# A two-layer encoder trunk on one core: small on-chip tiles allocated next to each other, so that the large tiles share one start residue modulo 512 bytes

## The chip, the cores and the metric

The kernel runs on one core of a Trainium2 chip, as one program with one launch. The metric is device microseconds for the whole program, median of three runs. TensorE (PE) multiplies, ScalarE (ACT) and VectorE (DVE) prepare and post-process, GpSimd (POOL) does a few small operations, and SyncE (SP) issues most DMAs. All tiles that the engines share lie in the on-chip memory SBUF, 128 partitions wide. An address in this text is the byte at which a tile starts inside each partition, and its residue is that address modulo 512.

## What is computed

Two layers (`L = 2`), sequence 256, width 2048. Each layer normalises `x`, projects it by a 2048 x 14784 matrix, runs four branches on the columns, and merges them:

```
for l in range(DEPTH):
    h = _rms_norm(x, norm_g[l])
    p = h @ w_in[l]
    ...                                  # split p into the inputs of four branches
    y_a = _rwkv7_bidir(...)              # bidirectional recurrent mixing
    y_b = _diff_attention(...)           # differential attention with a bias by distance
    y_c = _mla(...)                      # attention from low-rank latents
    y_d = _mem_attention(m_q, rms_norm(mem) @ mem_w_kv[l], ...)
    for bi, y in enumerate((y_a, y_b, y_c, y_d)):
        zb = sigmoid(merges[:, :, bi]) * ((y * silu(gates[:, :, bi])) @ w_branch[l, bi])
        z = zb if z is None else z + zb
    x = x + z @ w_out[l]
```

All of it is in float32, so the large products are made in three parts (below).

## The kernel before

**Main stream.** `main` (L564) walks a fixed list of jobs (`jobs`, L491). A job is one block of at most 512 weight columns: `mem_w_kv`, `w_in` (30 blocks), the latent up-projections, `w_branch`, `w_out`. For every 128 rows of a block, `prepare` loads the weights into `raww` (three buffers of 4096 bytes, two row groups each; SP issues the DMA), and `split` (L166) makes two float32r tiles from it: ACT copies to `whi`, DVE subtracts to `wlo` (five buffers each of 512 columns, 2048 bytes). The activations are split in the same way, once per use: `T1h`/`T1l` (high and low part of the normalised `x`, 16 slices of 256 columns), `ygh`/`ygl` (branch outputs), `S0` to `S7` (memory tokens), and for `w_out` a set of eight tiles that hold `z` in slices, in the order `X`, `iA`, `BK` with `qr`, `q1`, `T1h`, `k1`, `T1l`, `V1` (`z_prep`, L797). `product` (L624) then issues three matmuls: high x high, high x low, low x high.

**Which operand stays and which streams.** In most jobs (`tpos` false) the activation slice, 128 x 128, is loaded as the stationary operand, and 512 weight columns stream past it. In the jobs for the recurrent inputs and the gates (`tpos` true) a 128 x 128 slice of the weights is stationary, and 256 activation columns stream. A stationary slice is 512 bytes per partition, so that all slices of a tile start at the tile's own residue. In the trace the name before the comma is the streamed tile, the one behind it the stationary one: `mm<-whi,T1h` streams `whi` past a slice of `T1h`. The trace leaves the number off names, so `q` is `q1` and `k` is `k1`.

**Side work.** The branches, the norms and the tables run as generators that `build` (L1496) interleaves with the main stream by estimated engine clocks; their float32 matmuls go to the PSUM tags `pa` and `pr`.

**Where tiles lie.** A pool places tags in the order in which each is first used, one behind the other, each rounded up to 32 bytes. Before the change small tags lie between large ones: `small` (6 buffers of 64 bytes), `gains` (128 bytes), `cols` (476), `mrs` (8), `xss` (32), `bm` (256). `small(n)` (L181) hands out one of its buffers for row sums and softmax statistics; `rsqrt` (L176) runs on POOL with the constant -0.5 from `cst`.

| tile (use) | bytes | start before | residue before | start in the changed build | residue |
|---|---|---|---|---|---|
| whi, wlo (weights) | 2048 each | 91072 to 109504 | 448 | 91776 to 110208 | 128 |
| raww | 4096 each | 78784 | 448 | 79488 | 128 |
| T1l, T1h, V1 | 16384, 16384, 4096 | 112032, 135584, 151968 | 416 | 112256, 135808, 152192 | 128 |
| X, S0 to S7, ygh | 4096 each, 5120 | 20288, 24384, 69440 | 320 | 21120, 25216, 70272 | 128 |
| q1 | 4096 | 74688 | 448 | 75392 | 128 |
| k1, iA, BK, ygl, qr | 4096, 4096, 2048, 5120, 2048 | 181984, 199392, 197344, 203488, 220896 | 224 | 181888, 199296, 197248, 203392, 220800 | 128 |

Of the kernel before, what the change touches and what calls it, by code (L numbers as in the profile page):

```python
# [10 lines left out]
F32 = mybir.dt.float32  # L11
F32R = mybir.dt.float32r
I32 = mybir.dt.int32
U8 = mybir.dt.uint8
# [12 lines left out]
O_U, O_DQ, O_DK, O_DV, O_LAT, O_MQ, O_G, O_M = 0, 1792, 2304, 2816, 3328, 4032, 4544, 6592  # L27


C_ID, C_MF, C_MB, C_BLK, C_CEN, C_B2, C_MH, C_IF, C_OH, C_N = (  # L30
    0, 128, 256, 384, 512, 640, 642, 658, 690, 694)


P_SH, P_W0, P_A0, P_KK, P_KA, P_RK, P_GG, P_GB = 0, 42, 50, 58, 62, 66, 70, 74
P_DQ, P_DK, P_DS, P_QL, P_KL, P_NP, P_MM, P_N = 78, 79, 80, 81, 84, 86, 88, 90
# [18 lines left out]
def _constants():  # L54
    c = np.zeros((128, C_N), np.float32)
    c[:, C_ID:C_ID + 128] = np.eye(128)
    s = np.arange(128)[:, None] % 64
    t = np.arange(64)[None, :]
    c[:, C_MF:C_MF + 64] = s < t
    c[:, C_MF + 64:C_MF + 128] = s <= t  # L60
    c[:, C_MB:C_MB + 64] = s > t
    c[:, C_MB + 64:C_MB + 128] = s >= t
    blk = (np.arange(128)[:, None] // 64 == np.arange(128)[None, :] // 64).astype(np.float32)
    c[:, C_BLK:C_BLK + 128] = blk
    c[:, C_CEN:C_CEN + 128] = np.eye(128) - blk / 64
    c[:, C_B2:C_B2 + 2] = blk[:, [0, 64]]
    c[:, C_MH:C_MH + 16] = -0.5
    c[:, C_IF:C_IF + 32] = (10000.0 ** (-np.arange(0, 64, 2) / 64.0))[None, :]
    p = np.arange(128)
    g = p // 16 % 4  # L70
    c[p, C_OH + np.where(p < 64, g, 3 - g)] = 1.0
    return c
# [40 lines left out]
class Builder:  # L113
# [65 lines left out]
        self.nc.gpsimd.tensor_tensor(ss, ss, self.cst[:, C_MH:C_MH + n], op=ALU.pow)  # L179

    def small(self, n):  # L181
        return self.t("small", [128, 16], bufs=6)[:, :n]


    def setup(self):
        nc, a = self.nc, self.a
        self.cst = self.cp.tile([128, C_N], F32, name="cst")
        self.ident = self.cst[:, C_ID:C_ID + 128]
        self.G = [self.cp.tile([128, 2, 4, 65], F32, name=f"G{i}") for i in range(2)]
        self.ticks = [nc.gpsimd.memset(self.G[0], 1.0).ins]  # L190
        self.ones = self.cp.tile([128, 2], F32, name="ones")
        nc.gpsimd.memset(self.ones, 1.0)
        with self.tc.high_priority(2 * HP):
            nc.scalar.activation(self.small(2), self.ones, AF.Exp)
            warm = self.t("PT", [128, 2, 256], bufs=1)[:, 0]
            nc.vector.memset(warm, 0.0)
            ps = self.pa()[:, :256]
            for i in range(4):
                self.nc.tensor.matmul(ps, lhsT=warm[:, :128], rhs=warm, start=True, stop=True)
        self.TT = [self.cp.tile([128, 2, 4, 64], F32, name=f"TT{i}") for i in range(2)]  # L200
        self.ticks.append(nc.gpsimd.memset(self.TT[0], 0.0).ins)
        self.ST = [[self.cp.tile([128, 2, 2, 64], F32, name=f"ST{u}{i}") for i in range(2)] for u in range(2)]
        for s in self.ST[0]:
            at = nc.gpsimd.memset(s, 0.0).ins
        self.ticks.append(at)
        pace = self.t("X", [128, 1024])
        for i in range(6):
            with self.tc.issue_after(self.ticks[-1]):
                self.ticks.append(nc.gpsimd.memset(pace[:, i % 2 * 512:i % 2 * 512 + 512], 0.0).ins)
        with self.tc.issue_after(self.ticks[-1]):  # L210
            nc.gpsimd.memset(self.G[1], 1.0)
            for s in (self.TT[1], *self.ST[1]):
                nc.gpsimd.memset(s, 0.0)
        self.biasd = self.dr.tile([4, 128, 2, 256], F32, name="biasd")
        self.x1d = self.dr.tile([128, 2, 2048], F32, name="x1d")
# [925 lines left out]
    def rw_prep(self, l, ft, U, pos):  # L1141

        nc, a = self.nc, self.a
        cols = self.v["cols", l]
        cst = self.cst
# [3 lines left out]
        def col(p):  # L1149
            return cols[:, p:p + 1]  # L1150

        b2 = cst[:, C_B2:C_B2 + 2]
        wup = self.t("wup", [128, 2, 128], bufs=1)
        aup = self.t("aup", [128, 2, 128], bufs=1)
        fs = slice(ft * 128, ft * 128 + 128)
# [41 lines left out]
        for d in range(2):  # L1197
# [48 lines left out]
            for n in range(3):  # L1246
                c = 3 - n if d else n
# [99 lines left out]
    def rw_finish(self, l, ft, U, unit):  # L1347

        nc, cst = self.nc, self.cst
        cols = self.v["cols", l]  # L1350
        v = U[:, 8 + ft]
        kds, sq, yg = unit[4], *unit[-2:]
        b2 = cst[:, C_B2:C_B2 + 2]

        def col(p):
            return cols[:, p:p + 1]

        ps = self.pr()
        for tt in range(2):
            self.mm(ps[:, 2 * tt:2 * tt + 2], sq[:, tt * 128:tt * 128 + 128], b2)  # L1360
        var = self.small(4)
        nc.vector.tensor_scalar(var, ps[:, 0:4], 1.0 / 64, GN_EPS, op0=ALU.mult, op1=ALU.add)
        nc.gpsimd.tensor_tensor(var, var, cst[:, C_MH:C_MH + 4], op=ALU.pow)
        yield
        ex = self.t("sq", [128, 4, 64])
        nc.vector.tensor_copy(ex, var[:, :, None].to_broadcast([128, 4, 64]))
        bs = self.pr()[:, :256]
        self.mm(bs, cst[:, C_BLK:C_BLK + 128], kds)
        bv = self.t("r4", [128, 256], bufs=1)
        nc.vector.tensor_tensor(bv, bs, v, op=ALU.mult)  # L1370
        yield
        ps = self.pr()[:, :256]
        for tt in range(2):
            self.tr(ps[:, tt * 128:tt * 128 + 128], ex[:, 2 * tt:2 * tt + 2].rearrange("p a b -> p (a b)"))
        nc.vector.scalar_tensor_tensor(yg, yg, col(P_GG + ft), ps, op0=ALU.mult, op1=ALU.mult)
        nc.vector.scalar_tensor_tensor(U[:, ft], yg, col(P_GB + ft), bv, op0=ALU.add, op1=ALU.add)
        yield
# [250 lines left out]
```

## Time and profile before

| | |
|---|---|
| time of the kernel, median of 3 runs | 2039.71 us (2037.15 to 2041.34) |
| time of the profiled execution | 2037.85 us |
| its span, first to last instruction | 2036.1 us |
| PE busy | 2012.8 us, 99% of the span |
| DVE, ACT, POOL busy | 1433.0, 1114.3, 147.9 us |
| DMA traffic | 367 MB, 180 GB/s over the span |

A matmul row gives a modelled duration, since matmuls overlap: one of 512 columns is listed with some 395 ns, yet the next starts some 233 ns later. The pace of PE is therefore read from start to start, in the timeline, and not from the durations. In the timeline a line with x2 or x3 stands for that many instructions of one kind that follow each other, and its first number is the start of the first.

### The profile page before, as it was taken

To read this page: it belongs to the slowest core of one execution; us is meant where nothing else is said; L and a number is where in the kernel's file an instruction comes from. 1 tells how busy PE (TensorE), PEld (TensorE's weight loads), DVE (VectorE), ACT (ScalarE), POOL (GpSimd) and SP (SyncE) were. 2 spreads that over 40 slices of the span, in tenths; PEclk is the share of its full clock that TensorE was granted. 3 is DMA by queue.
4 is the path that set the end of the run, shared out by engine and by line. 5 is a ranking of instruction groups with operands and counts; after the bars stand their busy time and mean duration, and the time that the engine had idled before them with its cause. 6 is when DMAs were issued, how large, how long until landed. Compare 5 with 4: busy or idle time off the path is not lost.

```text
span 2036.1 us, 33810 instructions
## 1 busy us (share of the span) xinstructions
PE 2012.8 (99%) x12054; PEld 1688.6 (83%) x12054; DVE 1433.0 (70%) x3134; ACT 1114.3 (55%) x2293; POOL 147.9 (7%) x178
## 2 busy tenths in 40 slices
PE   9899999999999999999999999999999999999999
PEld 7798997778877877888889989987788878788887
DVE  6888898877787865648565658775577777565564
ACT  6756576455455544555465565755555554454443
POOL 1101112001100000100000000110011100000000
PEclk9899999999999999999999999999999999999999
DMA  8555655545565655765766656564556555456565
GB/s 275 181 177 160 196 179 179 171 136 159 166 203 168 181 164 158 222 189 191 243 191 181 186 151 192 166 194 140 151 172 187 173 169 180 150 168 200 185 197 187
DMA packets 222313, 367.34 MB, mean 180 GB/s; under 512 B 40576, under 2 KB 60800, under 8 KB 221824
## 3 DMA queue, kind: packets, MB, share of 16 engines
q1 hardware_dynamic: 218752, 356.31, 57.6%
q10 hardware_dynamic: 3168, 8.39, 1.1%
q8 instruction: 94, 1.54, 0.3%
q0 software_dynamic: 224, 0.49, 0.2%
q14 instruction: 75, 0.61, 0.1%
HBM read 357.78 MB, written 11.53 MB: 181 GB/s over the span
## 4 chain that ended last, share of the span: by engine, by line
PE 92%; DMA 3%; DVE 3%; issue 1%; ACT 1%; SPq 0%; POOL 0%; DVEq 0%; ACTq 0%; POOLq 0%
PE mm L156 82%; PE pr L156 5%; PE pa L156 2%; PE pa L161 2%; DVE wlo L95 1%; DMA raww<-in_w_in 1%; DMA raww<-in_mem_w_kv 1%; PE pr L161 0%; ACT whi L95 0%; DMA TT<-yd 0%; DVE half L95 0%; DVE BK L95 0%; DVE U L95 0%; DMA sc<-S 0%; DVE sq L95 0%
## 5 line engine op out<-in xcount | busy, mean ns | idle before, releaser
L95 DVE TENSOR_TENSOR wlo<-raww,whi 128x512 fp32r<-128x512 f32 (+2 forms) x1300 | 863.9, 674 | 468.8 <-ACT whi L95 463.8
L95 ACT ACTIVATE whi<-raww 128x512 fp32r<-128x512 f32 (+2 forms) x1300 | 789.7, 617 | 731.1 <-PE mm L156 538.0
L156 PE MATMUL mm<-whi,T1l 128*128 128x512 f32 (+2 forms) x1472 | 573.4, 392 | 0.0
L156 PE MATMUL mm<-wlo,T1h 128*128 128x512 f32 (+2 forms) x1440 | 569.6, 396 | 1.3 <-DVE wlo L95 1.1
L156 PE MATMUL mm<-whi,T1h 128*128 128x512 f32 (+2 forms) x1472 | 533.3, 394 | 1.6 <-ACT whi L95 1.6
L156 PEld LDWEIGHTS mm<-whi,T1h 128*128 128x128 f32 x1472 | 274.9, 188 | 62.8 <-ACT whi L95 2.3
L156 PEld LDWEIGHTS mm<-whi,T1l 128*128 128x128 f32 x1472 | 276.4, 188 | 58.6 <-issue 0.7
L156 PEld LDWEIGHTS mm<-wlo,T1h 128*128 128x128 f32 x1440 | 270.2, 188 | 62.5 <-DVE wlo L95 3.9
L156 PE MATMUL mm<-T1l,whi 128*128 128x256 f32 x960 | 271.9, 284 | 4.7 <-DVE T1l L95 4.7
L156 PE MATMUL mm<-T1h,whi 128*128 128x256 f32 x960 | 271.6, 284 | 2.3 <-ACT T1h L95 2.3
L156 PE MATMUL mm<-T1h,wlo 128*128 128x256 f32 x960 | 272.2, 285 | 0.4 <-DVE wlo L95 0.4
L156 PEld LDWEIGHTS mm<-T1l,whi 128*128 128x128 f32 x960 | 182.4, 190 | 5.6 <-DVE T1l L95 5.0
L156 PEld LDWEIGHTS mm<-T1h,whi 128*128 128x128 f32 x960 | 182.3, 190 | 3.1 <-ACT T1h L95 2.5
L156 PEld LDWEIGHTS mm<-T1h,wlo 128*128 128x128 f32 x960 | 182.0, 190 | 1.0 <-DVE wlo L95 0.8
L156 PE MATMUL mm<-wlo,ygh 128*128 128x512 f32 (+1 forms) x296 | 117.0, 397 | 0.0
L156 PE MATMUL mm<-whi,ygl 128*128 128x512 f32 (+1 forms) x296 | 115.7, 392 | 0.0
L156 PE MATMUL mm<-whi,ygh 128*128 128x512 f32 (+1 forms) x296 | 112.7, 400 | 0.0
L156 PE MATMUL mm<-whi,S 128*128 128x512 f32 x256 | 84.9, 408 | 2.6 <-ACT whi L95 2.1
L179 POOL TENSOR_TENSOR small<-small,cst 128x4 f32<-128x4 f32 (+3 forms) x45 | 52.0, 1157 | 395.1 <-DVE small L95 375.7
L156 PEld LDWEIGHTS mm<-whi,ygh 128*128 128x128 f32 x296 | 55.4, 188 | 12.3 <-issue 0.7
L156 PEld LDWEIGHTS mm<-whi,ygl 128*128 128x128 f32 x296 | 55.7, 188 | 11.9 <-issue 0.3
L156 PEld LDWEIGHTS mm<-wlo,ygh 128*128 128x128 f32 x296 | 55.7, 188 | 11.2 <-issue 0.7
(319 smaller groups left out, 2173.0 us busy)
## 6 DMA issues: line engine op xcount, KB each, us to landing
raww<-in_w_in SPq DMA_DIRECT2D x432, 512.0 KB, 3.6
raww<-in_w_branch SPq DMA_DIRECT2D x64, 512.0 KB, 4.3
raww<-in_w_out SPq DMA_DIRECT2D x64, 512.0 KB, 4.5
raww<-in_mem_w_kv SPq DMA_DIRECT2D x29, 512.0 KB, 4.2
raww<-in_w_in SPq DMA_DIRECT2D x16, 384.0 KB, 3.3
raww<-in_w_in SPq DMA_DIRECT2D x16, 320.0 KB, 3.6
raww<-in_w_in SPq DMA_DIRECT2D x16, 256.0 KB, 2.7
Z<-in_mem ACTq DMA_DIRECT2D x2, 1024.0 KB
```

The source lines that it names most:

```text
L95: return g(out, *args, **kw)
L156: return self.nc.tensor.matmul(out, lhsT=lhsT, rhs=rhs, start=start, stop=stop).ins
L161: self.nc.tensor.transpose(out, in_, self.ident[:k, :k])
L179: self.nc.gpsimd.tensor_tensor(ss, ss, self.cst[:, C_MH:C_MH + n], op=ALU.pow)
```

## The change

The constant tile `cst` loses two columns that held a pair of 0/1 block columns (`b2`, now read from the block matrix with a step of 64 columns) and eight of the sixteen columns of -0.5. It shrinks from 694 to 684 columns. `small` has five buffers in place of six. In `setup` the tags `gains`, `cols`, `mrs`, `xss` and `bm` and the first `small` are requested once, before any large tile, and so they lie together ahead of `PT`. From `PT` on, every tile starts at residue 128.

```
-C_ID, C_MF, C_MB, C_BLK, C_CEN, C_B2, C_MH, C_IF, C_OH, C_N = (
-    0, 128, 256, 384, 512, 640, 642, 658, 690, 694)
+C_ID, C_MF, C_MB, C_BLK, C_CEN, C_MH, C_IF, C_OH, C_N = (
+    0, 128, 256, 384, 512, 640, 648, 680, 684)
...
-    c[:, C_B2:C_B2 + 2] = blk[:, [0, 64]]
-    c[:, C_MH:C_MH + 16] = -0.5
+    c[:, C_MH:C_MH + 8] = -0.5
...
     def small(self, n):
-        return self.t("small", [128, 16], bufs=6)[:, :n]
+        return self.t("small", [128, 16], bufs=5)[:, :n]
...
         nc.gpsimd.memset(self.ones, 1.0)
+
+        for tag, n, dt in (("gains", 32, F32), ("cols", P_N + 29, F32), ("mrs", 2, F32), ("xss", 8, F32),
+                           ("bm", 256, U8)):
+            self.t(tag, [128, n], dt)
+        self.small(2)
...
-        b2 = cst[:, C_B2:C_B2 + 2]
+        b2 = cst[:, C_BLK:C_BLK + 128:64]
```

The last edit stands in `rw_prep` and in `rw_finish`. The tiles requested in `setup` have no instruction of their own. In the built programs each engine issues the same instructions in the same order before and after, with the same operands by name; only the DMA of `cst` is 10 columns shorter. PE, DVE and SP also wait for the same things at the same places. On ACT and POOL 37 waits differ, all at instructions that write a `small` tile or follow one that does, since five buffers come round sooner than six.

## Rows read from the trace of the kernel before

**Rows 1.** The page, part 1: engine, busy us (share), instructions.

```profile
PE 2012.8 (99%) x12054; PEld 1688.6 (83%) x12054; DVE 1433.0 (70%) x3134; ACT 1114.3 (55%) x2293; POOL 147.9 (7%) x178
```

**Rows 2.** The page, part 4: the chain that ended last, by engine and line.

```profile
PE 92%; DMA 3%; DVE 3%; issue 1%; ACT 1%; SPq 0%; POOL 0%; DVEq 0%; ACTq 0%; POOLq 0%
PE mm L156 82%; PE pr L156 5%; PE pa L156 2%; PE pa L161 2%; DVE wlo L95 1%; DMA raww<-in_w_in 1%; DMA raww<-in_mem_w_kv 1%; PE pr L161 0%; ACT whi L95 0%; DMA TT<-yd 0%; DVE half L95 0%; DVE BK L95 0%; DVE U L95 0%; DMA sc<-S 0%; DVE sq L95 0%
```

**Rows 3.** Waits: who waited for whom, us in total, times, longest.

```profile
ACT whi L95 <- PE mm L156: 538.0, 671, 3.7
...
ACT whi L95 <- DMA raww<-in_w_in: 99.0, 74, 5.3
...
ACT E L95 <- DVE small L95: 28.0, 19, 5.2
```

**Rows 4.** Groups by shape: line engine op, out<-streamed,stationary, xcount | busy us, mean ns | idle.

```profile
L156 PE MATMUL mm<-whi,T1l 128*128 128x512 f32 x1344 | 531.7, 399 | 0.0
L156 PE MATMUL mm<-wlo,T1h 128*128 128x512 f32 x1312 | 526.5, 401 | 1.3 <-DVE wlo L95 1.1
L156 PE MATMUL mm<-whi,T1h 128*128 128x512 f32 x1344 | 493.4, 400 | 0.9 <-ACT whi L95 0.9
...
L156 PE MATMUL mm<-T1h,wlo 128*128 128x256 f32 x960 | 272.2, 285 | 0.4 <-DVE wlo L95 0.4
...
L156 PE MATMUL mm<-wlo,ygh 128*128 128x512 f32 x272 | 109.0, 401 | 0.0
L156 PE MATMUL mm<-whi,ygl 128*128 128x512 f32 x272 | 107.2, 395 | 0.0
L156 PE MATMUL mm<-whi,ygh 128*128 128x512 f32 x272 | 105.0, 405 | 0.0
L156 PE MATMUL mm<-whi,S 128*128 128x512 f32 x256 | 84.9, 408 | 2.6 <-ACT whi L95 2.1 <-ACT S L95 0.4
...
L156 PE MATMUL mm<-wlo,S 128*128 128x512 f32 x128 | 52.3, 409 | 0.0
```

**Rows 5.** Timeline, PE in layer 0's `w_out`: start us, us, engine line op, names, xcount.

```profile
946.91 0.62 PE L156 MATMUL mm<-whi,q 128*128 128x512 f32 x2
...
949.64 0.63 PE L156 MATMUL mm<-whi,T1h 128*128 128x512 f32 x2
...
953.32 0.62 PE L156 MATMUL mm<-whi,k 128*128 128x512 f32 x2
...
963.10 0.64 PE L156 MATMUL mm<-whi,X 128*128 128x512 f32 x2
963.58 0.40 PE L156 MATMUL mm<-wlo,X 128*128 128x512 f32 x1
...
967.30 0.63 PE L156 MATMUL mm<-whi,BK 128*128 128x512 f32 x2
...
970.10 0.62 PE L156 MATMUL mm<-whi,q 128*128 128x512 f32 x2
...
972.85 0.63 PE L156 MATMUL mm<-whi,T1h 128*128 128x512 f32 x2
```

**Rows 6.** Groups by shape, PE, 936.7 to 1043 us (layer 0's `w_out`).

```profile
L156 PE MATMUL mm<-whi,X 128*128 128x512 f32 x32 | 10.9, 395 | 0.0
...
L156 PE MATMUL mm<-whi,k 128*128 128x512 f32 x32 | 10.7, 394 | 0.0
L156 PE MATMUL mm<-whi,q 128*128 128x512 f32 x32 | 10.6, 391 | 0.0
```

**Rows 7.** Timeline, PE in a job that streams 256 activation columns.

```profile
123.89 0.28 PE L156 MATMUL mm<-T1l,whi 128*128 128x256 f32 x1
...
126.97 0.28 PE L156 MATMUL mm<-T1h,whi 128*128 128x256 f32 x1
```

**Rows 8.** Groups by shape, DVE.

```profile
L95 DVE TENSOR_TENSOR wlo<-raww,whi 128x512 fp32r<-128x512 f32 x1192 | 812.0, 690 | 435.1 <-ACT whi L95 430.6
...
L95 DVE TENSOR_TENSOR Z<-Z,sg 128x512 f32<-128x512 f32 x32 | 22.2, 692 | 0.2
```

**Rows 9.** The tile `sq`: the matmuls with `b2`, duration ns min/median/max.

```profile
L156 PE MATMUL pr<-cst,sq x32: 165/251/272, 140.3 to 1604.5; 128*128 128x2 f32 x32
```

More of the change, by code (lines that the diff above doesn't have):

```diff
@@ L1352, in rw_finish @@
         kds, sq, yg = unit[4], *unit[-2:]
-        b2 = cst[:, C_B2:C_B2 + 2]
+        b2 = cst[:, C_BLK:C_BLK + 128:64]
         def col(p):
```

## The prediction

> **What bounds the kernel now.** I read the busy table first: PE is busy 99% of the span, DVE 70%, ACT 55% [rows 1]. Since matmul durations are modelled, that alone doesn't show a bound, so I went on to the chain of work that ended last: 92% of it is PE, and 82% is the one line that issues the weight products [rows 2]. The waits say the same from the other side: the longest in total is ACT's, 538.0 us for a `whi` buffer that PE hasn't released yet [rows 3]. The weights are ready ahead of PE nearly everywhere. So the time is the number of products by the distance from one start to the next, and a change that moves neither instructions nor waits on PE can act only through that distance. The reader should therefore look at the start times of the products, and at what tells a slow distance from a fast one.
>
> **What the starts show.** In `w_out` the same `whi` and `wlo` tiles stream past eight sets of stationary slices in turn, 12 products a set, all of one shape and with no wait. From the first product of `k` to the first of `BK` there are five sets (`k`, `T1l`, `V`, `X`, `iA`), 60 products, in 967.30 - 953.32 = 13.98 us [rows 5], or 233.0 ns each. The set of `q` takes 949.64 - 946.91 = 2.73 us, and in the next pass 972.85 - 970.10 = 2.75 us [rows 5]: 227.5 and 229.2 ns each, 228.3 on average. The modelled durations of that stage agree in sign: 391 ns for `q`, 394 for `k`, 395 for `X` [rows 6]. What sets `q1` apart is its address: it alone begins at residue 448, the residue of `whi` and `wlo` that stream past it. The five others begin at 416, 320 and 224, and whichever of these it is, the set comes out at about 233. I read this as the two reads of PE, the stream of the current product and the load of the next stationary slice, getting in each other's way a little unless both start at the same place modulo 512. After the change every product has such a pair.
>
> **The change, part by part.**
>
> Products of 512 columns. The eight rows of this shape hold 1344 + 1312 + 1344 + 3 x 272 + 256 + 128 = 5,200 [rows 4]. `w_out` has 2 layers x 4 blocks x 16 slices x 2 halves x 3 = 768; 160 of them already stand in the rows of `T1h` and `T1l`, and 96 are those of `q1`, which have equal residues already. That leaves 5,200 + 768 - 160 - 96 = 5,712 products that change. Each should go from 233.0 to 228.3 ns: 4.7 ns x 5,712 = 26.8 us. Ends: 3 ns by the modelled durations of `q` and `k` [rows 6], 17 us; 5.5 ns by the better pass of `q`, 31 us.
>
> Products of 384 and 320 columns (456 in the latent blocks) have the same operands and shorter streams: 1 us.
>
> Products of 256 columns: 3 x 960 = 2,880 [rows 4]. Here the weight slice, residue 448, is stationary, and `T1h` or `T1l`, residue 416, streams. 26 of them start within 126.97 - 123.89 = 3.08 us [rows 7], 118.5 ns each. No row shows this shape with equal residues. At the share of the long ones (4.7 of 233.0, 2%) they would save 2.4 ns each, 6.9 us; at the least they save nothing, and at the most the same 4.7 ns, 13.5 us. A loss can't be excluded by a row either (the rival below prices it). I take half of the share, 1.2 ns, 3.5 us.
>
> The rest. DVE and ACT may read and write at any of these residues: DVE's operation of 512 elements takes 690 ns where all three tiles lie at 448 and 692 ns where they lie at 448 and 224 [rows 8], so that sharing a residue costs or gives DVE nothing. The two-column matmuls with `b2` number 32, at a median of 251 ns [rows 9]; reading their two columns 256 bytes apart may change them by some tens of ns each, 1 us together either way, beside work of other lanes. I take 0. With five `small` buffers, 37 waits on ACT and POOL differ. Nothing is queued on PE behind them directly; behind an ACT one stands the next `whi`, and PE holds whole `whi` buffers ahead (the 538.0 us). All of ACT's waits of softmax exponentials for DVE's statistics are 28.0 us in total today [rows 3]; if that grew by a tenth, 3 us on ACT, PE would see little of it. I take 0, and 3 us as its end. The shorter DMA of `cst` is nothing.
>
> What comes late next. The gain is 26.8 + 1 + 3.5 = 31 us, 1.5% of PE's pace. ACT has 45% of the span free and DVE 30% [rows 1], so they can follow. Some waits remain and don't shrink: 8% of the chain is not PE [rows 2], among it DMA at 3%, and ACT waits 99.0 us for weights still on their way [rows 3]. Where such a wait ends last, a faster PE only arrives earlier. I take a tenth of the gain back, 3 us: 28 us remain.
>
> Sum, against the profiled execution: 2037.85 - 28 = 2010. It lies 1.9 us under the median of the runs shown, so the time I give is 2012. Its own ends: a gain of 17 less a fifth is 14 us, 2026; a gain of 31 + 1 + 13.5 is 45 us, 1994.
>
> **A rule against it.** The starts differ by 4.7 ns between `q1` and the rest [rows 5], in the same stage, with the same streamed tiles. The Trainium skill (SBUF — State Buffer, Who interferes with whom) says that PE has two independent read ports, one for the moving operand and one for LDWEIGHTS, and that PE never waits on anyone. By that rule the residue is worth nothing and the time stays at 2040; by the row it is worth 28 us. The trace speaks against the rule, as far as one tile out of eight can.
>
> **The rivals.**
>
> No change. Then `q1` would be fast for another reason: it lies next to `raww` and nearer to `whi` than any other set does, or the order of the sets favours it. For it: only one tile of eight has equal residues, and it has one place. Against it: `wlo` lies 10 KB further than `whi`, and both kinds of product sit in the sets that I timed; `X`, `V` and `k` lie at very different distances and are alike. The products keep 233 ns and `small` and `b2` remain: 2037 to 2042, say 2040. By the page's rule above it comes out here as well. Chance 0.21.
>
> Slower. Equal residues keep the two reads in step for the whole stream, and in step could mean in conflict every time. The rows hold such a pace: two products of `X` take 963.58 - 963.10 = 0.48 us, 240 ns each [rows 5]. At 240 in place of 233, 5,712 products cost 40 us more: 2080. It decides as soon as the mean distance of the 512-column products is above 233.0. Against it stands `q1`, which has equal residues and the lowest pace; for it, that the residue itself will be 128 and no longer 448, which no pair of the trace has. With a 240 on a part of the products only, it ends between 2044 and 2080. Chance 0.14.
>
> Given back. PE's pace improves as forecast, but the feed of weights takes half of it: ACT already waits 74 times for `raww` from `w_in` [rows 3], with only three `raww` buffers. 2037.85 - 15 + 1.9 = 2025. Against it: the 538.0 us in which ACT waits for PE are five times as much. Chance 0.10.
>
> **How the numbers follow.** The forecast, 2012 with its own ends 1994 and 2026, gets 0.55. Forecast and half gain together make faster 0.65. No change is 0.21; slower is 0.14. About 0.2% (4 us) is what a measurement of this kernel can tell from no change. The range reaches from 1994 over the half gain to the no-change case at 2042, and leaves out the slower case (0.14) and a few hundredths below.
>
> **What would show it.** In the profile after, every set of `w_out` should take 2.72 to 2.76 us from its first product to the first of the next, and no longer only `q`'s; the groups of 512 columns should be listed some 3 to 5 ns shorter, `T1h` and `T1l` above all; the 256-column products should start 116 to 118.5 ns apart; DVE's 690 ns should stay. If the sets still take 2.79 while `q` does too, the residue was not the cause and the rival of no change holds. If `q` stays fast and the others don't follow, equal residues are not enough. If the sets take 2.73 and the time stays, the gain was given back, and ACT's waits for `raww` must have grown.

## The result and the profile after

The changed kernel takes **2016.39 us** (median of 4 runs, 2015.58 to 2017.52) against 2038.82 us of the kernel before (median of 4 runs beside it, 2037.15 to 2041.34): a ratio of 0.9889, 95% interval 0.9872 to 0.9906. The forecast was 2012, faster. The profiled execution took 2015.58 us, 22.3 us less than that of before; its span fell by the same amount, from 2036.1 to 2013.8 us.

The page of the kernel after, busy line and chain, as [rows 1] and [rows 2]. Line numbers are one lower than before (L155 is the matmul that was L156):

```profile
PE 1990.4 (99%) x12054; PEld 1693.6 (84%) x12054; DVE 1431.4 (71%) x3134; ACT 1111.5 (55%) x2293; POOL 149.2 (7%) x178
...
PE 93%; DVE 3%; DMA 2%; issue 1%; ACT 0%; POOL 0%; SPq 0%; DVEq 0%; ACTq 0%; POOLq 0%
```

The instruction counts are the same, PE is as full as before, and PE's busy time alone is 22.4 us shorter. Nothing was taken off the chain; its steps became shorter. The waits of after, as [rows 3] (who waited for whom: us in total, times, longest):

```profile
ACT whi L94 <- PE mm L155: 406.1, 496, 6.5
...
ACT whi L94 <- DVE wlo L94: 132.5, 180, 1.7
...
ACT whi L94 <- DMA raww<-in_w_in: 98.6, 73, 3.8
...
ACT E L94 <- DVE small L94: 29.1, 19, 5.4
...
PE mm L155 <- ACT whi L94: 3.2, 4, 1.5
```

Two of these rows before, which [rows 3] does not show:

```profile
ACT whi L95 <- DVE wlo L95: 21.1, 28, 2.1
...
PE mm L156 <- ACT whi L95: 3.8, 4, 1.5
```

ACT's wait for PE to release a `whi` is 132 us shorter, but 111 us of that stand under DVE's `wlo` now: the profile puts a wait for several engines down to the one that came last. The rows of PE and of `wlo` together went from 559.1 to 538.6 us, 20.5 less. PE itself waits for `whi` and `wlo` 4.6 us in total (5.3 before), so the feed still keeps up. ACT's wait for `raww` from `w_in` (99.0 before) and the one for `small` (28.0 before) have hardly moved; over all weights, ACT's waits for `raww` went from 134.1 to 140.8 us.

PE in layer 0's `w_out` after, as [rows 5] (start us, us, engine line op, names, xcount):

```profile
944.42 0.62 PE L155 MATMUL mm<-whi,k 128*128 128x512 f32 x2
...
958.02 0.62 PE L155 MATMUL mm<-whi,BK 128*128 128x512 f32 x2
...
960.74 0.62 PE L155 MATMUL mm<-whi,q 128*128 128x512 f32 x2
...
963.46 0.62 PE L155 MATMUL mm<-whi,T1h 128*128 128x512 f32 x2
```

From the first product of `k` to the first of `BK` the same 60 products take 13.60 us where they took 13.98: 226.7 ns each, not 233.0. The set of `q` takes 2.72 us and no longer stands out. The groups by shape after, as [rows 4] (us in total, modelled mean ns):

```profile
L155 PE MATMUL mm<-whi,T1l 128*128 128x512 f32 x1344 | 525.5, 394 | 0.0
...
L155 PE MATMUL mm<-T1h,wlo 128*128 128x256 f32 x960 | 274.5, 287 | 0.0
...
L155 PE MATMUL mm<-whi,ygl 128*128 128x512 f32 x272 | 106.4, 392 | 0.0
...
L155 PE MATMUL mm<-whi,S 128*128 128x512 f32 x256 | 82.3, 399 | 2.5 <-ACT whi L94 2.5
```

The groups of 512 columns in [rows 4] lost 3 to 10 ns by their modelled durations, those with `S` most. The group of 256 columns **gained** 2 ns. The timeline of a job with 256 columns after, as [rows 7], says the same by its starts: 26 products in 127.03 - 123.91 = 3.12 us, 120.0 ns each, where it was 118.5.

```profile
123.91 0.28 PE L155 MATMUL mm<-T1l,whi 128*128 128x256 f32 x1
...
127.03 0.28 PE L155 MATMUL mm<-T1h,whi 128*128 128x256 f32 x1
```

DVE's operation of 512 elements and the 32 matmuls with `b2`, as [rows 8] and [rows 9], did not move (690 ns and 251 ns before):

```profile
L94 DVE TENSOR_TENSOR wlo<-raww,whi 128x512 fp32r<-128x512 f32 x1192 | 811.5, 691 | 420.0 <-ACT whi L94 415.6 <-PE mm L155 0.5
```
```profile
L155 PE MATMUL pr<-cst,sq x32: 165/251/272, 138.1 to 1589.1; 128*128 128x2 f32 x32
```

**The whole account.** A mean *pace* in the rest of this text is the distance from the start of a product to the next start on PE, over all products of one width that are followed directly by another product. Distances above 256 ns (512 columns) or 128 ns (256 columns), 5% and 3% of them, are left out as interrupted. Number of distances, their sum and their mean:

| | 512 columns | 256 columns |
|---|---|---|
| before | 5,317, 1238.5 us, 232.9 ns | 2,759, 326.4 us, 118.3 ns |
| after | 5,312, 1210.4 us, 227.9 ns | 2,750, 329.6 us, 119.9 ns |

So 28.1 us went out of the long products and 3.2 us came back in the undisturbed short ones (1.6 ns on all 2,880 are 4.5 us). All starts from product to whatever follows add up to 1832.2 us before and 1808.4 after, 23.8 less. The span fell by 22.3, so 1.5 us came back outside the products.

### The profile page after: what moved, and what is told of

It is laid out like the page before. It is cut to its first block, busy times and chain, and to the rows that moved or that the text cites. A ratio compares the mean times of both kernels' runs of the same rounds, so it can differ in the third digit from the quotient of the medians.

```text
span 2013.8 us, 33812 instructions
## 1 busy us (share of the span) xinstructions
PE 1990.4 (99%) x12054; PEld 1693.6 (84%) x12054; DVE 1431.4 (71%) x3134; ACT 1111.5 (55%) x2293; POOL 149.2 (7%) x178
## 3 DMA queue, kind: packets, MB, share of 16 engines
q10 hardware_dynamic: 3168, 8.39, 1.2%
## 4 chain that ended last, share of the span: by engine, by line
PE 93%; DVE 3%; DMA 2%; issue 1%; ACT 0%; POOL 0%; SPq 0%; DVEq 0%; ACTq 0%; POOLq 0%
PE mm L155 84%; PE pr L155 5%; PE pa L155 3%; PE pa L160 2%; DVE wlo L94 1%; DMA U<-in_memT 1%; DMA raww<-in_mem_w_kv 0%; PE pr L160 0%; DMA TT<-yd 0%; DVE BK L94 0%; DMA raww<-in_w_in 0%; DMA BK<-sp 0%; DVE half L94 0%; ACT whi L94 0%; DVE U L94 0%
## 5 line engine op out<-in xcount | busy, mean ns | idle before, releaser
L155 PE MATMUL mm<-whi,T1l 128*128 128x512 f32 (+2 forms) x1472 | 567.2, 388 | 0.0
L155 PE MATMUL mm<-wlo,T1h 128*128 128x512 f32 (+2 forms) x1440 | 564.8, 392 | 1.4 <-DVE wlo L94 1.4
L155 PE MATMUL mm<-whi,T1h 128*128 128x512 f32 (+2 forms) x1472 | 527.8, 391 | 0.7 <-ACT whi L94 0.7
L155 PEld LDWEIGHTS mm<-whi,T1h 128*128 128x128 f32 x1472 | 275.3, 188 | 55.9 <-ACT whi L94 2.0
L155 PEld LDWEIGHTS mm<-whi,T1l 128*128 128x128 f32 x1472 | 276.9, 188 | 51.8 <-issue 0.7
L155 PEld LDWEIGHTS mm<-wlo,T1h 128*128 128x128 f32 x1440 | 270.8, 188 | 58.1 <-DVE wlo L94 5.3
L155 PE MATMUL mm<-T1l,whi 128*128 128x256 f32 x960 | 274.1, 286 | 4.7 <-DVE T1l L94 4.7
L155 PE MATMUL mm<-T1h,whi 128*128 128x256 f32 x960 | 273.8, 286 | 2.3 <-ACT T1h L94 2.3
L155 PE MATMUL mm<-T1h,wlo 128*128 128x256 f32 x960 | 274.5, 287 | 0.0
L155 PEld LDWEIGHTS mm<-T1l,whi 128*128 128x128 f32 x960 | 185.9, 194 | 5.5 <-DVE T1l L94 5.0
L155 PEld LDWEIGHTS mm<-T1h,whi 128*128 128x128 f32 x960 | 185.8, 194 | 3.0 <-ACT T1h L94 2.5
L155 PEld LDWEIGHTS mm<-T1h,wlo 128*128 128x128 f32 x960 | 185.5, 194 | 0.4
L155 PE MATMUL mm<-wlo,ygh 128*128 128x512 f32 (+1 forms) x296 | 116.0, 393 | 0.0
L155 PE MATMUL mm<-whi,ygl 128*128 128x512 f32 (+1 forms) x296 | 114.9, 389 | 0.0
L155 PE MATMUL mm<-whi,ygh 128*128 128x512 f32 (+1 forms) x296 | 111.7, 397 | 0.0
L155 PE MATMUL mm<-whi,S 128*128 128x512 f32 x256 | 82.3, 399 | 2.5 <-ACT whi L94 2.5
L155 PEld LDWEIGHTS mm<-whi,ygh 128*128 128x128 f32 x296 | 55.3, 188 | 11.4 <-issue 0.7
L155 PEld LDWEIGHTS mm<-whi,ygl 128*128 128x128 f32 x296 | 55.6, 188 | 11.0 <-issue 0.3
L155 PEld LDWEIGHTS mm<-wlo,ygh 128*128 128x128 f32 x296 | 55.6, 188 | 10.6 <-issue 0.7
```

What stands on the lines that cost most here:

```text
L155: return self.nc.tensor.matmul(out, lhsT=lhsT, rhs=rhs, start=start, stop=stop).ins
```

## Experiments

The theory to be tested: PE's pace in the 512-column products is set by the difference between the start residues of the weights and of the other operand. Below, **D** is the residue at which the weights start minus that of the other tile, modulo 512. Before, D is 32 for `T1h`, `T1l` and `V1`, 128 for `X`, `S` and `ygh`, 224 for `k1`, `iA`, `BK`, `qr` and `ygl`, and 0 for `q1` alone. After, it is 0 everywhere. The rivals: that one of the other edits (`small`, `b2`, `cst`) does it, or the residue 128 itself.

**E1, the placement alone**, in the kernel before: six `small`, the long `cst` and the old `b2` stay; every large tile comes to residue 224, not 128.

```
         nc.gpsimd.memset(self.ones, 1.0)
+        for tag, n, dt in (("gains", 32, F32), ("cols", P_N + 29, F32), ("mrs", 2, F32), ("xss", 8, F32),
+                           ("bm", 256, U8)):
+            self.t(tag, [128, n], dt)
+        self.small(2)
```

> The kernel before with the six requests in setup alone: six small buffers, the long constants and the two columns of b2 stay. Every tile from PT on then starts at residue 224, which is not a multiple of 64. Theory (the difference between the residue of the streamed tile and that of the stationary tile sets the pace): 512-column products start 226 to 228 ns apart in all eight sets of w_out, and the time is that of the changed kernel, 2016 us, within 3. Rival (the residue 128 itself, or starts on multiples of 128 bytes): the pace stays at 233 ns and the time at 2039 us. Rival (small, constants or b2 did it): 2039 us too.

Measured: 2019.42 us (2018.37 to 2022.86), 0.9906 of before [0.9889, 0.9922]; 227.8 and 119.9 ns. PE in `w_out` of this kernel:

```profile
948.68 0.62 PE L156 MATMUL mm<-whi,k 128*128 128x512 f32 x2
...
962.28 0.62 PE L156 MATMUL mm<-whi,BK 128*128 128x512 f32 x2
```

60 products in 13.60 us, as in the kernel after. The time is 0.4 us beyond the expected band, but the ratio agrees with that of the kernel after (0.9889 [0.9872, 0.9906]). The gain is in the placement, and the residue 128 has no part in it.

**E2, all the rest**: the kernel after without the five lines above, so that every D is as before.

```
-        for tag, n, dt in (("gains", 32, F32), ...):
-            self.t(tag, [128, n], dt)
-        self.small(2)
```

> The changed kernel without the requests in setup: five small buffers, short constants, b2 read with a step. All tiles from PT on move by the same 96 bytes against before, so that their residues differ as before (streamed weights 352, q1 352, T1h 320, X 224, k1 128). Theory: sets of w_out at 233 ns a product, q alone near 228, 2039 us within 3. Rival (small, constants or b2 did it): 2016 us.

Measured: 2039.73 us, 0.9996 of before [0.9985, 1.0007]; 233 and 118.3 ns. In its `w_out`:

```profile
950.50 0.62 PE L155 MATMUL mm<-whi,q 128*128 128x512 f32 x2
...
953.23 0.63 PE L155 MATMUL mm<-whi,T1h 128*128 128x512 f32 x2
...
956.91 0.62 PE L155 MATMUL mm<-whi,k 128*128 128x512 f32 x2
...
970.89 0.63 PE L155 MATMUL mm<-whi,BK 128*128 128x512 f32 x2
```

13.98 us for the 60 products and 2.73 us for `q`, both as before. The residue of every large tile has moved by 96 bytes, no difference has, and `q` is still the one fast set. `small`, `b2` and `cst` are worth nothing that can be measured.

**E3 and E4, ten differences in one kernel.** On top of the kernel after, each of the ten weight buffers gets its own tag and starts 32 bytes further in its residue than the one ahead of it. In E3 the `whi` have D = 0 to 128 and the `wlo` 160 to 288; in E4, 192 to 320 and 352 to 480. One `Rs` in place of two makes the room.

```
+        if FIRST:
+            self.t("skip", [128, 8 * FIRST])          # FIRST = 0 (E3), 6 (E4)
+        for i in range(10):
+            self.t(("whi", "wlo")[i // 5] + "ABCDE"[i % 5], [128, 512], F32R)
+            if i < 9:
+                self.t("gap" + "ABCDEFGHI"[i], [128, 8])
...
-                hi = self.t("whi", [128, 512], F32R, bufs=self.LOOK)
-                lo = self.t("wlo", [128, 512], F32R, bufs=self.LOOK)
+                c = "ABCDE"[nxt[0] % 5]
+                hi = self.t("whi" + c, [128, 512], F32R)
+                lo = self.t("wlo" + c, [128, 512], F32R)
```

> The changed kernel, with the ten buffers of whi and wlo as ten tiles that start 32 bytes further each: the streamed weights lie 0, 32, 64, 96, 128 (whi A to E) and 160, 192, 224, 256, 288 bytes (wlo A to E) past the residue 128 of all other tiles. Rs has one buffer in place of two, for room. Theory with modulus 512: only whiA streams at 227 ns, all others at 229 to 236. If the modulus is 256, wloD at 256 is at 227 too; if 128 or 64, also whiE, or whiC. Rival (neighbourhood, not difference): no pattern by letter. For the 256-column products, where these tiles are stationary, before (difference 32) gave 118 ns and the changed kernel (0) 120: whiB at about 118, whiA at 120, the others open. Time between 2020 and 2045 us.

> As the sweep before, with the weights 192, 224, 256, 288, 320 (whi A to E) and 352, 384, 416, 448, 480 bytes (wlo A to E) past the residue of all other tiles. Theory: no equal pair, so 229 to 236 ns for 512 columns everywhere unless 256 counts as equal (whiC). A difference of 480 is 32 the other way round: if only its size counts, wloE behaves as whiB of the other sweep. For 256 columns: open, 116 to 122 ns. Time between 2030 and 2050 us.

Measured: 2035.09 and 2032.38 us (one run each). The expectation for `whiA` failed. It has D = 0 in E3, but its products go at 232.9 ns; one set of six, from its first start to that of the next buffer (PE, `w_out`):

```profile
952.76 0.63 PE L156 MATMUL mm<-whiA,T1h 128*128 128x512 f32 x2
...
954.16 0.63 PE L156 MATMUL mm<-whiB,k 128*128 128x512 f32 x2
```

1.40 us for six. Streams of `whiA` and `wloA` (D = 160) alternate in it. All other 512-column paces of the two kernels lie between 230.0 and 233.7 ns, too. For 256 columns `whiA` was expected near 120 ns and has 118.4. So the theory of one product's own pair of tiles falls as it stood. Mended: it takes a row of products with the same D before the fast pace shows.

**E5, one difference per job.** Weight buffers of 2560 bytes, four of each kind and not five; every job uses the 2048 bytes that begin 0, 32, ... or 480 bytes in, and its tiles get a letter, A for D = 0 to P for D = 480. Within a job, D is constant.

```
-    LOOK = 5
+    LOOK = 4
...
+        for j in jobs:
+            j.off = 8 * (seen[j.tpos] * 7 % 16)
+            seen[j.tpos] += 1
...
+                c = "ABCDEFGHIJKLMNOP"[j.off // 8]
+                hi, lo = (self.sb.tile([128, 640], F32R, name=f"{t}{c}_{self.n}", tag=t, bufs=self.LOOK)
+                          [:, j.off:j.off + 512] for t in ("whi", "wlo"))
```

> The changed kernel with weight buffers of 2560 bytes, four of each kind in place of five (the same room), in which each job uses the 2048 bytes that begin 0, 32, 64 ... 480 bytes in (letters A to P): within one job all streamed and all stationary tiles keep one difference of residues, and it differs from job to job. Theory as mended after the two sweeps (the pace is steady and best when all reads in a row begin at the same residue, and the two sweeps mixed streams of ten residues): jobs A at 226 to 227 ns for 512 columns, all other letters 229 to 236, and A at 120 ns for 256 columns, B near 118 as in the kernel before (there the weights lie 32 past T1). If only the difference to the stationary slice counted and the mixing were harmless, A would be at 227 here but the first sweep's whiA (232.9 ns) would stay unexplained. If equality modulo 256 or 128 is enough, I (256), or E and M as well, are at 227. Rival (something else in the two sweeps spoiled the pace): A above 230. The time itself says little, since four buffers in place of five bring waits: 2030 to 2080 us.

Measured: 2045.64 us in one run. Mean pace in ns by D:

| D | 0 | 32 | 64 | 96 | 128 | 160 | 192 | 224 | 256 | 288 | 320 | 352 | 384 | 416 | 448 | 480 |
|---|---|---|---|---|---|---|---|---|---|---|---|---|---|---|---|---|
| 512 columns | 228.8 | 233.2 | 229.3 | 233.4 | 232.4 | 234.1 | 233.1 | 233.0 | 228.2 | 233.2 | 229.1 | 233.6 | 232.7 | 233.9 | 233.4 | 233.5 |
| 256 columns | 119.9 | 118.3 | 117.8 | 118.0 | 118.6 | 119.7 | 117.8 | 116.8 | 119.8 | 118.3 | 114.7 | 117.8 | 118.6 | 119.7 | 115.7 | 116.7 |

Two jobs that follow each other, K (D = 320) and B (D = 32), PE's timeline, same stationary tiles:

```profile
880.67 0.62 PE L155 MATMUL mm<-whiK,T1h 128*128 128x512 f32 x2
...
893.03 0.62 PE L155 MATMUL mm<-whiK,T1h 128*128 128x512 f32 x2
894.41 0.63 PE L155 MATMUL mm<-whiB,T1h 128*128 128x512 f32 x2
...
902.80 0.63 PE L155 MATMUL mm<-whiB,T1h 128*128 128x512 f32 x2
```

Nine steps of six products in 12.36 us are 228.9 ns each for K; six steps in 8.39 us are 233.1 for B. The mended theory holds: within a job, the pace of 512 columns is that of its D. D = 0 and 256 are fastest, 64 and 320 nearly so, all others near 233. The 256-column products want something else: D = 0 and 256 are their worst case (with 160 and 416), and 320 has the lowest mean. Letters B (D = 32, as before the change) and A (D = 0, as after it) have the 118.3 and 119.9 ns of the two kernels, so both signs of the result are found again. At one D their pace can even take two values. In letter K, 42 products take 561.05 - 556.28 = 4.77 us, 113.6 ns each, while in another part of the job 12 take 542.58 - 541.17 = 1.41 us, 117.5 ns each:

```profile
541.17 0.28 PE L155 MATMUL mm<-T1h,wloK 128*128 128x256 f32 x1
...
542.58 0.28 PE L155 MATMUL mm<-T1h,wloK 128*128 128x256 f32 x1
```
```profile
556.28 0.28 PE L155 MATMUL mm<-T1h,wloK 128*128 128x256 f32 x1
...
561.05 0.28 PE L155 MATMUL mm<-T1h,wloK 128*128 128x256 f32 x1
```

A mean by letter therefore depends on which value the rows of that one job took. The job of letter C (D = 64) ran at the slower one, 117.8 ns, throughout; that D = 64 is slower than D = 320 is not shown by it.

**E9 and E6, D = 256 and D = 320 for all weights.** The kernel after, with its instructions in the same order; some of the small tiles go directly ahead of the weights and an unused tile behind them, so that only the weights move.

```
                if nxt[0] == 0:
                    self.t("bm", [128, 256], U8)           # E9; E6: mrs, xss and bm, 320 bytes
                hi = self.t("whi", [128, 512], F32R, bufs=self.LOOK)
                lo = self.t("wlo", [128, 512], F32R, bufs=self.LOOK)
                if nxt[0] == 0:
                    self.t("pad", [128, 64])               # E6: 48
```

> The kernel after, with the same instructions in the same order, but all ten weight buffers begin 256 bytes further (residue 128) than every other large tile (residue 384), by one small request ahead of the weights and 256 unused bytes behind them. Theory of the residue modulo 256 (from the jobs of letter I, at 228.2 ns as letter A): products of 512 columns at 226.7 to 228.5 ns, of 256 columns at 119.9 ns, time 2016 us (2014 to 2019). Rival, that the whole 512 bytes must agree and letter I had its pace from something else: 232 to 233 ns as in the kernel before and 2036 to 2041 us.

> The kernel after, with the same instructions in the same order, but all ten weight buffers begin 320 bytes further (residue 128) than every other large tile (residue 320). Theory that the pace is a function of this one difference, as read by job: products of 512 columns 229.1 to 229.3 ns (letters C and K; +1.3 to +2 ns on 5,712 products = +7 to +11 us against after), products of 256 columns 114.7 ns (letter K; -5.2 ns on 2,880 = -15 us), together 4 to 8 us under the kernel after: 2008 to 2012 us. Rival, that only equal residues keep a pace and letter K's numbers were those of the jobs that got it: 232 to 233 ns and 118 ns, 2036 to 2041 us.

E9: 2018.74 us, 0.9895 of before [0.9880, 0.9909]; 227.8 and 119.9 ns, the paces of the kernel after. Equality modulo 256 is enough. From `k` to `BK` in its `w_out`, 60 products take 13.60 us again:

```profile
948.06 0.62 PE L155 MATMUL mm<-whi,k 128*128 128x512 f32 x2
...
961.66 0.61 PE L155 MATMUL mm<-whi,BK 128*128 128x512 f32 x2
```

E6: 2017.09 us (2015.58 to 2017.32), 0.9886 of before [0.9869, 0.9902]; 229.3 and 116.1 ns. The 60 products take 13.74 us, 229.0 ns each; by shape, the 256-column group is at 282 ns, where the kernel after has 286:

```profile
944.65 0.62 PE L155 MATMUL mm<-whi,k 128*128 128x512 f32 x2
...
958.39 0.62 PE L155 MATMUL mm<-whi,BK 128*128 128x512 f32 x2
```
```profile
L155 PE MATMUL mm<-T1h,whi 128*128 128x256 f32 x960 | 269.7, 282 | 2.3 <-ACT T1h L94 2.3
```

Both signs came as expected, the size of the second did not, and the time missed the expected 2008 to 2012: the pace is 116.1, not 114.7, since both values of the 256-column pace occur. Against the kernel after, 1.4 ns x 5,712 = 8 us are lost and 3.8 ns x 2,880 = 11 us won; 3 us are about what the medians of such runs scatter, and the ratio is that of the kernel after. E6 is no better kernel, but it moves the two widths in opposite directions with no instruction moved.

**E7 and E8, each width at its better D.** Buffers as in E5; in E7 the `tpos` jobs (256 columns) use D = 320, all others 0. E8, the control, uses 0 throughout.

```
+                a0 = 80 if j.tpos else 0                  # E8: 0
+                hi, lo = (self.t(x, [128, 640], F32R, bufs=self.LOOK)[:, a0:a0 + 512] for x in ("whi", "wlo"))
```

> Four buffers of 2560 bytes for each half of the weights in place of five of 2048 (a look-ahead of 4 pieces, not 5); the jobs whose products have 256 columns use the 2048 bytes that begin 320 in, all other jobs the first 2048, so that products of 512 columns have equal residues and those of 256 columns a difference of 320. Read against the run with the same four buffers and no shift: products of 512 columns unchanged at 227 ns, of 256 columns 114.7 in place of 119.9 ns, so 15 us less (12 to 17). Rival, that a change of residue between jobs costs as much as it gives: within 3 us of that run.

> The control of the mixed kernel: four buffers of 2560 bytes for each half of the weights, every job uses the first 2048 bytes, so that all residues are equal as in the kernel after. The job-by-job kernel with these buffers took 2045.6 us, while its paces (512 columns 232.2 ns and 256 columns 118.0 ns on average over the letters) stand 4.9 x 5,712 = 28 us above and 1.9 x 2,880 = 5.5 us below those of the kernel after, which makes 2039; so the shorter look-ahead should cost 7 us: 2023 us (2020 to 2027), at 227 and 120 ns. Rival, that those 7 us were the switches of residue between its jobs: 2016 us (2014 to 2018).

E8: 2034.05 us (2028.93 to 2038.82), 0.9969 [0.9947, 0.9991]; 227.9 and 119.8 ns. The look-ahead of four costs more than the expected 7 us, some 18 by the medians and 13 by the two profiled executions. PE's matmuls also stand in another order than in the kernel after, so the look-ahead alone is not measured; E7 and E8 have the same order. E7: 2024.40 us (2023.81 and 2024.99), 0.9924 [0.9904, 0.9943]; 227.9 and 115.6 ns. One row of the 256-column groups by shape, E7 and then E8:

```profile
L155 PE MATMUL mm<-T1h,whi 128*128 128x256 f32 x960 | 267.0, 282 | 3.6 <-ACT T1h L94 3.6
```
```profile
L155 PE MATMUL mm<-T1h,whi 128*128 128x256 f32 x960 | 271.3, 286 | 3.7 <-ACT T1h L94 3.6
```

The undisturbed 256-column distances sum to 316.0 us in E7 and 328.5 in E8, 12.5 us less, near the expectation. All starts together fall by 6.2 us only (1818.8 against 1825.0), the profiled executions by 5.1. The other half came back, mostly in interrupted distances: those of 256 columns grew from 26.3 to 30.8 us. Here half of a gain is given back, as in a rival of the prediction, in a kernel whose look-ahead is short. But ACT's waits for `raww` are no longer (118.6 against 118.1 us in all); what grew is PE's wait for `whi` and `wlo`, from 15.2 to 18.2 us.

**E10 and E11, the same with a look-ahead of five.** The room is found by putting each half of the weights in one ring of five pieces, with 192 bytes more, and by one `Rs` in place of two. In the ring a new piece overwrites an old one, and in the steps that take one output block after the other the old one's products for the second block are still to come; those products use newer weights, and their number and shape are unchanged.

```
+                    rings = [self.t("whi", [128, 2608], F32R)]
+                    self.t("pad", [128, 80])
+                    rings.append(self.t("wlo", [128, 2608], F32R))
+                a0 = nxt[0] % self.LOOK * 512 + (0 if j.tpos else 48)    # E11: + 48
+                hi, lo = (x[:, a0:a0 + 512] for x in rings)
```

> Both paces at once, with the look-ahead of 5 kept: each half of the weights in one ring of five pieces of 2048 bytes and 192 bytes more; the jobs with products of 256 columns use the ring from its start (320 bytes beyond the residue of every other large tile), all other jobs 192 bytes further (equal residues). One buffer of Rs in place of two makes the room; the scheduler puts some work in another order. Theory, by the paces of the four-buffer kernels: products of 512 columns 227.9 ns, of 256 columns 115.6 in place of 119.8 ns, 4.2 x 2,880 = 12 us less than the ring without the change of residue, and 2004 us (2002 to 2010) if ring and order cost nothing. Rival, that ring, order and the one buffer of Rs cost as much as the shorter look-ahead did (12 us and more): 2016 us or above.

> The control of the ring: every job uses the ring from 192 bytes in, so that all residues are equal; products of 512 and 256 columns at 227.9 and 119.8 ns as in the kernel after, time 2016 us (2014 to 2022) if ring, order and the one buffer of Rs cost little. Rival: 2028 us and above, as with the shorter look-ahead.

E10: 2074.04 us, 1.0166 of before [1.0144, 1.0189]; E11: 2058.89 us, 1.0082 [1.0056, 1.0107]. The paces are as expected (228.1 and 115.8 ns, 228.0 and 119.8 ns), but the rival holds: the scheduler orders much of the work otherwise around a ring, and interrupted distances of 512 columns take 151.9 and 131.2 us, where they took 96.2 in the kernel after. PE waits 40.5 and 25.4 us for `whi` and `wlo`, where it waited 4.6. So no kernel of this study beats the one after. A mixed placement with the look-ahead of five in separate buffers would need 5,120 bytes, where 384 are free; it was not tried.

## Why the prediction was right, and where not

**The reading that carried it.** One tile of eight with equal residues had the fast pace, and the forecast extended it to all. E1 shows that the placement is the cause of the gain, E9 and E6, where only the weights move, that it is their D, and E2 that the rest is worth nothing, as the prediction put it. The rival of no change (some other property of `q1`) falls by both: in E2 `q` is alone in being fast after all addresses have moved, in E1 all sets are. By the rule of the Trainium skill that the prediction set against itself (SBUF — State Buffer, Who interferes with whom: two independent read ports, PE never waits), E1 should have stayed at 2040 us; it took 2019.42. For products of this kind the measurement decides against that reading of the rule, that the residue is worth nothing; whether the two ports are what meets is not shown.

**Products of 512 columns.** Forecast: 4.7 ns x 5,712 = 26.8 us. The undisturbed distances fell by 5.1 ns on average; x 5,712 this is 29 us, inside the ends of 17 and 31. The two passes of `q` that gave 228.3 ns were a little slower than the sets are now (226.7), because a set is short. In the second pass its twelve distances are 223, 232, 236, 228, 233, 230, 227, 227, 226, 227, 227 and 235 ns: the pace settles within the set, and the last distance, up to the first product of `T1h`, is slow again. In the kernel after, too, the first nine distances of an undisturbed row (one without a left-out distance or another matmul in it) are 227.6 to 233.5 ns on average by their place, and only from the tenth on 226.7; before, they stay between 231 and 234 at every place. That `q`'s mean lay so near the mean of all products after (227.9) was in part luck, since short rows are frequent there, too.

**Products of 256 columns: the step that failed.** I gave them a gain of 3.5 us, between 0 and 13.5, by the share of the long ones. They lost: 118.3 to 119.9 ns, 1.6 ns x 2,880 = 4.5 us. "A loss can't be excluded by a row either" was right, and the lower end of that term should have been below zero. The step took over the sign from a shape whose streamed and stationary operands have the opposite roles and whose width is another, and E5 shows that this shape has its own best D. Whether the roles or the width make the difference, no run tells; the products of 384 and 320 columns, which stream weights too, gained 0.3 ns at most. The sign to look for, starts 116 to 118.5 ns apart, failed with 120.0. This one term is 8 us off; the whole forecast for the profiled execution, 28 us, is 5.7 above the 22.3 measured.

**Products of 384 and 320 columns**: 174.8 to 174.7 and 146.7 to 146.3 ns, some 0.1 us in place of 1. **The rest** at nothing: E2, within 0.11% of 1.

**Given back.** Forecast: a tenth, 3 us. By the terms as measured, 29 + 0.1 - 4.5 = 24.6 us against 22.3 in the time, so 2 to 3 us. ACT's waits for `raww` grew by 7 us over all weights, but PE's wait for `whi` and `wlo` did not (5.3 to 4.6 us), so the half gain of the third rival did not come. The 538.0 us of ACT waiting for PE pointed the right way; of the room that they and the row of DVE's `wlo` show together, 20.5 us went, about the gain itself.

**Slower.** No set goes at 240 ns. The two products of `X` that gave that pace were part of a row at D = 128, whose mean is 233.

**What stays open** is the cause below the addresses. The runs show which D are fast for which shape, that the value of the residue doesn't matter (with D = 0 the paces are the same at 128, at 224 in E1 and at 320 in E11), and that a mixed row is slow. Whether the two reads of PE meet in SBUF, or something else counts from the start of a tile, no run here tells.

## What to carry to other kernels

Where PE is full and two sets of identical products differ by 2% in their starts, compare the start addresses of their operands: here the equality of two residues modulo 256 bytes was worth 1.1% of the time, for some lines that reserve small tiles early. Don't take a shape's result to a shape of another width, or with streamed and stationary operands exchanged; measure one job of each, with one difference per job, since a mixed row hides the effect. What is won on PE must then survive the feed: a shorter look-ahead, bought to place the weights better, cost more than the placement gave, together with the other order of work that came with it.

## What the runs showed of the hardware

- With D = 0 a product of 512 columns starts every 226.7 ns once nine others of its row have gone ahead, and one of 256 columns every 120.0 ns. The middle half of all distances lies between 226 and 227, and at 120; a fifth of those of 512 columns are 229 ns or more, most of them early in a row. At 2.4 GHz (granted clock 1.00 in the stretches shown) this is 544 and 288 cycles: 32 more than columns, in both shapes.
- The 512-column pace by D is near 227 to 229 ns at D = 0, 64, 256 and 320 and near 233 elsewhere; the pattern repeats after 256 bytes. The 256-column pace goes from 114.7 (D = 320) to 119.9 ns (D = 0). D = 64 and 320 differ there by 3 ns, but by the values that their rows took, so whether it repeats after 256 is open.
- The 256-column products ran at 113.6 or at 117.5 ns at one and the same D, and stayed at one of these for dozens of products. In E6, 28 of the 32 undisturbed rows of 15 or more keep one of two values, 113.4 or 117.8 ns, after their first three. What picks the value wasn't found.
